# Value products in groups of four key blocks, and one more step ahead of the transposition of the row maxima

## The chip, the cores and the metric

The kernel is written directly for the engines of one core of a Trainium2 chip. The metric is the time of one launch on the device in microseconds; 2396.0 us is the median of three runs before the change (2391.77 to 2398.43).

## The reference

One layer of a decoder block over 2048 tokens of width 1024. Two attention branches read the same normalised input, each is gated, projected, weighted and summed. What matters here is the dense part of both branches, cut to its core:

```python
def mla_attention(q, k, v):                    # branch A: 8 heads, 96 wide, values 64 wide
    sc = einsum('bqhd,bkhd->bhqk', qb, k) * scale
    sc = where(causal, sc, -inf)
    p = softmax(sc, axis=-1)
    return einsum('bhqk,bkhd->bqhd', p, v)

def dsa_attention(q, k, v, q_idx, k_idx, w_idx, k_top):   # branch B: 8 heads, 2 key heads, 64 wide
    score = einsum('bqhs,bqh->bqs', relu(q_idx . k_idx), w_idx)
    _, sel = top_k(where(causal, score, -inf), 256)
    p = softmax(q . k[sel] * scale)            # over the 256 selected keys
    return p . v[sel]
```

The kernel does not gather in branch B: it computes all scores of a query block and adds a mask that is very negative where a key was not selected.

## The kernel before

The first 1106 us project the tokens, score and search the 256 keys, and write queries, keys, values and gates to device memory. The last 388 us merge the branches and apply the output projection. The change lies between them, in the attention.

**Units.** Attention is cut into 32 units in the hand-written order `UNITS` (line 38). A unit is one branch, one pair of heads (p, 0 to 3) and one group of 512 queries (g, 0 to 3). It has `nk` = 4g + 4 key blocks of 128 keys, 4 to 16; in all there are 320 blocks. For a block, `scores_t` (lines 629 to 680) computes for each of the two heads the transposed scores `st` (128 keys by 512 queries, three products in branch A, two in branch B, and bf16 products that add masks), ScalarE takes the exponential into `pt` (line 672), and the sum of the exponentials is kept in `acc` by an addition on GpSimd for the first head and on VectorE for the second (line 679). The last four blocks of a unit lie on the diagonal, so they are 512, 384, 256 and 128 columns wide.

**Value products.** `values` (line 682) multiplies `pt` with the values into `o`. It is two matmuls for a block, one for each head, and each head fills 64 of the 128 output rows, so that two of them run beside each other. A profile shows each such matmul as two records. They are not issued with their block: `scores_t` hands them to a list, and `flush` (lines 740 to 752), which is called inside every block after its first score products (`between`), issues them later, in groups. Three tiles in PSUM hold `st`, three hold `ap` (below) and two hold `o`.

**The end of a unit.** `finish` (line 689) multiplies `o` with the gate on VectorE, and sums `acc` over its 128 rows by two matmuls with ones on TensorE (line 698), for which both heads' last additions must be done. `flush` calls it after the value products, so many acting flushes after the unit's end as `AGE` says.

**Maxima.** The softmax subtracts a row maximum that is known before the unit begins. For each unit, `row_max` (line 590) computes the scores a second time the other way round, in 8(g + 1) pieces of up to 512 keys: a product `ap` on TensorE (line 600), then a maximum over it on VectorE (line 604, in branch B line 607), then for each of 8 rows of results a negation into `nm` (line 614). `shifts` (line 616) then transposes `nm` on TensorE (line 623), and ScalarE copies it and sends it by DMA into the last row of `Q` or `Q2`, where the score products pick it up.

**The order.** TensorE's order is exactly the order in which this code emits instructions (`manual_schedule`); the other engines' queues are ordered by a scheduler. While a unit runs, `fill` (line 760) gives out pieces of the next two or three units between the score products, by a rate that spreads them over the blocks that are left. A `yield` in `row_max` or `shifts` ends one step; `left` counts a unit's steps, 8(g + 1) + 2 of them: the pieces, the step that ends the last row's maximum, and the transposition. The steps of units 0 and 1 are taken in `project_tail` (line 1147), 28 of them, between the last products of the projection.

Of the kernel before, what the change touches and what calls it, by code (L numbers as in the profile page):

```python
# [28 lines left out]
SELECTED = -4.0e30  # L29
TOPK = 256  # L30
TARGET = 248.0
AGE = 1
X_BUFS = 3
X_AHEAD = 4
FIRST_GEMMS = [(0, 0), (0, 1), (0, 2), (1, 0), (0, 3), (1, 1), (0, 4), (0, 5), (1, 2), (0, 6), (1, 3), (0, 7), (1, 4), (1, 5), (1, 6), (1, 7)]
# [11 lines left out]
TAIL = 3  # L47
WAIT = 0
LEAD = 6
PT_BUFS = 10  # L50
WINDOW = 8.5
EVALS = 5
PAIRS = [(NT - 1 - n, 2 + n) for n in range(7)]
# [18 lines left out]
class Block:  # L72
# [543 lines left out]
    def shifts(self, g, q, k, mask, dst):  # L616
        nc, hd = self.nc, self.hd
        nm = hd.tile([P, 2, 4], F32, name="nm", tag="nm", bufs=3)
        for hh in range(2):
            yield from self.row_max(g, q(hh), k(hh), mask, nm[:, hh])  # L620
        yield
        ps = self.ps.tile([P, 512], F32, name="ap", tag="ap", bufs=3)
        nc.tensor.transpose(ps[0:8, 0:P], nm.rearrange("p a b -> p (a b)"), self.ident)
        nmT = hd.tile([8, P], F32R, name="nmT", tag="t8", bufs=2)
        nc.scalar.activation(nmT, ps[0:8, 0:P], AF.Copy)
        nc.scalar.dma_start(dst.bitcast(F32), nmT.bitcast(F32))
        yield

    def scores_t(self, u, j, fill, between):
# [18 lines left out]
        for hh in range(2):  # L648
# [21 lines left out]
            ps = banks[hh]  # L670
            pt = at.tile([P, 512], F32, name="pt", tag="pt", bufs=PT_BUFS)
            nc.scalar.activation(pt[:, n0:], ps[:, n0:], AF.Exp, scale=u["scale"])  # L672
# [41 lines left out]
    def pipeline(self, units, ahead):  # L714
        count = len(units)
        heads, spec, left = [None] * count, [None] * count, [0] * count
        begun, born, clock = 0, [0] * count, [0]

        def begin(n):
            nonlocal begun  # L720
            while begun < count and begun - ahead[begun] <= n:
                m = begun
                heads[m] = units[m]()
                spec[m] = next(heads[m])
                left[m] = 8 * (spec[m]["g"] + 1) + 2
                born[m] = clock[0]
                begun += 1

        def take(n):
            left[n] -= 1  # L730
            next(heads[n])

        begin(-1)
        for n in range(2):
            while left[n]:
                take(n)
                yield
        values, after = [], []

        def flush(keep=1):  # L740
            nonlocal after
            if keep and len(values) < 3:
                return
            while len(values) > keep:
                f, u, j = values.pop(0)
                f(u, j)
            rest = []
            for age, f, u in after:
                again = (age - 1, f) if age else f(u)
                if again is not None:  # L750
                    rest.append((again[0], again[1], u))
            after = rest

        for n in range(count):
            begin(n)
            u = spec[n]
            credit = [0.0]
            for j in range(u["nk"]):

                def fill(half):  # L760
                    slots, pieces, rate = 2 * (u["nk"] - j) - half - LEAD, 0, 0.0
                    for m in range(n + 1, begun):
                        pieces += left[m]
                        rate = max(rate, pieces / max(slots, 1))
                        slots += 2 * spec[m]["nk"]
                    credit[0] += rate
                    for m in range(n + 1, begun):
                        while left[m] and credit[0] >= 1.0 and clock[0] >= born[m] + WAIT:
                            take(m)
                            credit[0] -= 1.0  # L770

                clock[0] += 1
                values.append((self.scores_t(u, j, fill, flush), u, j))
            after.append((AGE, self.finish, u))
            while n + 1 < count and left[n + 1]:
                take(n + 1)
        while values or after:
            flush(0)
# [466 lines left out]
```

## Time and profile before

| what | value |
|---|---|
| median of three runs | 2396.0 us |
| the profiled execution | 2390.5 us, of that 2388.7 us from the first to the last instruction |
| TensorE busy | 2271.3 us (95%) |
| VectorE / GpSimd / ScalarE busy | 1446.3 us (61%) / 1317.2 us (55%) / 992.1 us (42%) |
| granted TensorE clock | 0.987 of full speed over the span |
| attention | from about 1106.6 to 2000.6 us |

Durations below come from this one execution. A matmul's record lasts longer than its share of TensorE, since matmuls overlap; the share is read from start to start. PE is TensorE's matmul side, PEld its weight loads, DVE VectorE, ACT ScalarE, POOL GpSimd. In a timeline equal instructions that follow each other are merged into one row (x8 are eight records), and the number in brackets is the idle time of the engine before it and what ended it.

### The profile page before, as it was taken

To read this page: it belongs to the slowest core of one execution; us is meant where nothing else is said; L and a number is where in the kernel's file an instruction comes from. 1 tells how busy PE (TensorE), PEld (TensorE's weight loads), DVE (VectorE), ACT (ScalarE), POOL (GpSimd) and SP (SyncE) were. 2 spreads that over 40 slices of the span, in tenths; PEclk is the share of its full clock that TensorE was granted. 3 is DMA by queue.
4 is the path that set the end of the run, shared out by engine and by line. 5 is a ranking of instruction groups with operands and counts; after the bars stand their busy time and mean duration, and the time that the engine had idled before them with its cause. 6 is when DMAs were issued, how large, how long until landed. Compare 5 with 4: busy or idle time off the path is not lost.

```text
span 2388.7 us, 38186 instructions
## 1 busy us (share of the span) xinstructions
PE 2271.3 (95%) x12882; PEld 1759.2 (74%) x12882; DVE 1446.3 (61%) x3296; ACT 992.1 (42%) x2002; POOL 1317.2 (55%) x1733
## 2 busy tenths in 40 slices
PE   7999999999988999899999999999999999999999
PEld 6999988877777777786565655656655556888888
DVE  6453525698686887866676676677778763222222
ACT  5342325766657667442344434434434443111110
POOL 5876958866666767643344434334765445433431
PEclk9999999999999999999999999999999999999999
DMA  9441333443448434448433322211313103444432
GB/s 308 140 144 52 122 109 127 147 153 115 155 145 253 149 115 153 132 143 243 139 103 100 116 72 63 68 53 59 95 50 98 32 14 101 143 145 137 128 125 84
DMA packets 298102, 288.39 MB, mean 121 GB/s; under 512 B 23408, under 2 KB 240880, under 8 KB 297776
## 3 DMA queue, kind: packets, MB, share of 16 engines
q1 hardware_dynamic: 297392, 285.81, 38.8%
q8 instruction: 101, 1.65, 0.3%
q14 instruction: 97, 0.79, 0.1%
q10 hardware_dynamic: 512, 0.13, 0.0%
HBM read 171.62 MB, written 114.10 MB: 120 GB/s over the span
## 4 chain that ended last, share of the span: by engine, by line
PE 51%; DVE 12%; DMA 8%; issue 5%; POOL 5%; ACT 4%; SPq 2%; DVEq 0%; ACTq 0%; POOLq 0%
PE st L646 17%; PE o L686 10%; PE ap L600 5%; DMA out_dram<-mx 4%; PE acc L113 3%; PE acc L114 3%; DVE sc L392 3%; PE acc L115 3%; ACT junk L439 2%; PE br L113 2%; PE br L115 1%; PE br L114 1%; PE st L698 1%; DMA mo<-d_o 1%; ACT zr L389 1%
## 5 line engine op out<-in xcount | busy, mean ns | idle before, releaser
L679 POOL TENSOR_TENSOR acc<-acc,pt 128x512 f32<-128x512 f32 (+3 forms) x288 | 327.3, 1137 | 361.1 <-ACT pt L672 350.0
L672 ACT ACTIVATE pt<-st 128x512 f32<-128x512 f32 (+3 forms) x640 | 339.6, 533 | 433.5 <-PE st L646 385.0
L392 DVE SCALAR_TENSOR_TENSOR sc<-zr,w_i,sc 128x512 f32<-128x512 f32 (+3 forms) x266 | 227.9, 859 | 98.4 <-ACT zr L389 94.8
L646 PE MATMUL st<-Q,K 96*128 96x512 f32 (+3 forms) x960 | 264.9, 383 | 0.5 <-ACT ev L352 0.5
L607 DVE CUSTOM_DVE_ANT_0 mj<-ap,mask 128x512 bf16<-128x512 f32 (+2 forms) x320 | 193.7, 605 | 102.4 <-PE ap L600 93.8
L604 DVE TENSOR_REDUCE mx<-ap 128x1 f32<-128x512 f32 (+2 forms) x320 | 185.3, 604 | 109.8 <-PE ap L600 64.5
L679 DVE TENSOR_TENSOR acc<-acc,pt 128x512 f32<-128x512 f32 (+3 forms) x288 | 218.7, 759 | 51.1 <-ACT pt L672 46.4
L646 PEld LDWEIGHTS st<-Q,K 96*128 96x128 f32 (+1 forms) x960 | 163.2, 191 | 73.2 <-issue 50.8
L389 ACT ACTIVATE zr<-z 128x512 f32<-128x512 f32 (+3 forms) x304 | 161.7, 544 | 90.1 <-PE z L387 85.7
L113 PE MATMUL acc<-hT0h,wfh 128*128 128x512 f32 x384 | 155.8, 406 | 8.4 <-ACT pqk L560 6.4
L113 PE MATMUL acc<-hT1h,wfh 128*128 128x512 f32 x384 | 157.7, 411 | 5.8 <-DMA hT1h<-d_h 2.9
L108 POOL TENSOR_SCALAR wfh<-wst 128x256 fp32r<-128x256 f32 x192 | 91.4, 490 | 123.2 <-DMA wst<-in_w_f 64.9
L109 POOL TENSOR_TENSOR wfl<-wst,wfh 128x256 fp32r<-128x256 f32 x192 | 157.1, 835 | 3.1
L114 PE MATMUL acc<-hT1l,wfh 128*128 128x512 f32 x384 | 153.4, 400 | 0.8 <-DMA hT1l<-d_h 0.8
L115 PE MATMUL acc<-hT1h,wfl 128*128 128x512 f32 x384 | 153.2, 399 | 0.0
L114 PE MATMUL acc<-hT0l,wfh 128*128 128x512 f32 x384 | 151.8, 395 | 1.0 <-DMA hT0l<-d_h 1.0
L115 PE MATMUL acc<-hT0h,wfl 128*128 128x512 f32 x384 | 151.7, 395 | 0.0
L686 PE MATMUL o<-pt,V 128*64 128x512 f32 (+3 forms) x640 | 135.9, 546 | 0.0
L686 PE MATMUL o<-pt,Vb 128*64 128x512 f32 (+3 forms) x640 | 134.5, 541 | 0.0
L646 PE MATMUL st<-Q,Kd 128*128 128x512 f32 (+3 forms) x320 | 133.0, 416 | 0.0
L907 DVE TENSOR_TENSOR sg<-br,sg 128x256 f32<-128x256 f32 x128 | 53.5, 423 | 128.4 <-PE br L115 72.1
L106 ACT ACTIVATE mh<-sg 128x256 fp32r<-128x256 f32 x64 | 26.7, 416 | 251.6 <-POOL sg L909 251.5
(283 smaller groups left out, 6101.1 us busy)
## 6 DMA issues: line engine op xcount, KB each, us to landing
wst<-in_w_f SPq DMA_DIRECT2D x192, 128.0 KB
d_f<-ev SPq DMA_DIRECT2D x96, 256.0 KB
sg<-d_f SPq DMA_DIRECT2D x128, 128.0 KB
d_q<-phl SPq DMA_DIRECT2D x32, 384.0 KB
d_k<-phl SPq DMA_DIRECT2D x32, 384.0 KB
K<-d_k SPq DMA_DIRECT2D x64, 192.0 KB
Q<-d_q SPq DMA_DIRECT2D x64, 192.0 KB
x<-in_x SPq DMA_DIRECT2D x16, 512.0 KB
```

Source lines behind the costliest of these rows:

```text
L109: (eng_lo or eng).tensor_tensor(lo, src, hi.bitcast(F32), op=OP.subtract)
L113: mm(ps, lhi, rhi, start=start, stop=False)
L114: mm(ps, lhi, rlo, start=False, stop=False)
L115: mm(ps, llo, rhi, start=False, stop=stop)
L389: nc.scalar.activation(r[:, :n], z[:, :n], AF.Relu)
L392: nc.vector.scalar_tensor_tensor(sc[:, k0:k0 + n], r[:, :n], ws, sc[:, k0:k0 + n], op0=OP.mult, op1=OP.add)
L604: nc.vector.tensor_reduce(mx[:, b:b + 1], ps[:, :n], axis=AX, op=OP.max)
L607: nc.vector.tensor_tensor_reduce(out=junk[:, :n], in0=ps[:, :n], in1=mask[i][:, 512 * b:512 * b + n], scale=1.0, scalar=-3.0e38, op0=OP.su ...
L646: nc.tensor.matmul(banks[hh][:, cols], l, r, start=start and n == 0, stop=stop and n == len(seq) - 1)
L672: nc.scalar.activation(pt[:, n0:], ps[:, n0:], AF.Exp, scale=u["scale"])
L679: eng.tensor_tensor(acc[:, n0:], acc[:, n0:], pt[:, n0:], op=OP.add)
L686: self.nc.tensor.matmul(u["o"][64 * hh:64 * hh + 64, n0:], u["v"](hh, j), pts[hh][:, n0:], start=(j == 0), stop=(j == u["nk"] - 1))
```

## The change

`flush` acts once more than four blocks are in the list, instead of three, and again leaves one; so it issues four blocks' value products in a row instead of two, at every fourth block. `AGE` goes from 1 to 0: `finish` follows in the same flush the value products of the unit's last block. There are 13 tiles `pt` instead of 10. `shifts` has one more empty step between the end of the last maximum and the transposition, and `left` counts it.

```diff
-AGE = 1
+AGE = 0
-PT_BUFS = 10
+PT_BUFS = 13
+GROUP = 4
@@ shifts
             yield from self.row_max(g, q(hh), k(hh), mask, nm[:, hh])
         yield
+        yield
         ps = self.ps.tile([P, 512], F32, name="ap", tag="ap", bufs=3)
         nc.tensor.transpose(ps[0:8, 0:P], nm.rearrange("p a b -> p (a b)"), self.ident)
@@ pipeline, begin
-                left[m] = 8 * (spec[m]["g"] + 1) + 2
+                left[m] = 8 * (spec[m]["g"] + 1) + 3
@@ pipeline, flush
-            if keep and len(values) < 3:
+            if keep and len(values) <= GROUP:
                 return
             while len(values) > keep:
                 f, u, j = values.pop(0)
                 f(u, j)
```

All line numbers of the changed program are one or two higher (line 600 is 601, 686 is 688, 698 is 700). In its order TensorE has 80 runs of value products, where there were 160. Three places show how its queue moves.

The first is TensorE's queue in the last quarter of a unit of branch A with 16 blocks, ahead of the transposition for the next unit (`o<-pt,V` are value products, `ap<-K,Q` a piece, `ap<-ident,nm` the transposition). Before:

```order
L600 MATMUL ap<-K,Q 128x512
L602 LDWEIGHTS identb
L602 MATMUL ap<-trib,identb 128x128
L646 MATMUL st<-Q,K 128x512
L686 MATMUL o<-pt,V 64x512 x4
L646 MATMUL st<-Q,K 128x512 x5
L623 MATMUL ap<-ident,nm 8x128
L646 MATMUL st<-Q,K 128x512 x3
```

The same place in the changed program:

```order
L601 MATMUL ap<-K,Q 128x512
L603 LDWEIGHTS identb
L603 MATMUL ap<-trib,identb 128x128
L648 MATMUL st<-Q,K 128x512 x9
L625 MATMUL ap<-ident,nm 8x128
L648 MATMUL st<-Q,K 128x512 x3
```

The transposition stands three score products further from the last piece than it did, and the value products that stood between them have gone to another block. Of the 32 transpositions, 8 had value products between the last piece and themselves; now 2 have.

The second place is TensorE's queue at the end of a unit of four blocks in branch A (`st<-acc,ones` are the sums of `finish`). Before, the unit's last value products (64x256 and 64x128) stood fourteen rows higher than the first sum, and the sums stood behind the next unit's first value products:

```order
L600 MATMUL ap<-K,Q 128x512
L646 MATMUL st<-Q,K 128x512
L686 MATMUL o<-pt,V 64x512 x4
L698 MATMUL st<-acc_14482,ones 64x512
L698 MATMUL st<-acc_14483,ones 64x512
L646 MATMUL st<-Q,K 128x512 x2
```

Now the four blocks' products and the sums are one run, in the second block of the next unit:

```order
L601 MATMUL ap<-K,Q 128x512
L648 MATMUL st<-Q,K 128x512
L688 MATMUL o<-pt,V 64x512 x2
L688 MATMUL o<-pt,V 64x384 x2
L688 MATMUL o<-pt,V 64x256 x2
L688 MATMUL o<-pt,V 64x128 x2
L700 MATMUL st<-acc_14477,ones 64x512
L700 MATMUL st<-acc_14478,ones 64x512
L648 MATMUL st<-Q,K 128x512
```

The sums have moved two blocks forward, right behind the unit's own last value products.

The third place is TensorE's queue at the seam between projection and attention (`acc<-hT1h,wfh` and its like are products of the projection). Before:

```order
L600 MATMUL ap<-K,Q 128x512 x2
L602 LDWEIGHTS identb
L602 MATMUL ap<-trib,identb 128x128
L113 MATMUL acc<-hT1h,wfh 128x512
L114 MATMUL acc<-hT1l,wfh 128x512
L115 MATMUL acc<-hT1h,wfl 128x512
L113 MATMUL acc<-hT1h,wfh 128x512
L114 MATMUL acc<-hT1l,wfh 128x512
L115 MATMUL acc<-hT1h,wfl 128x512
L623 MATMUL ap<-ident,nm 8x128
```

In the changed program:

```order
L115 MATMUL acc<-hT1l,wfh 128x512
L116 MATMUL acc<-hT1h,wfl 128x512
L601 MATMUL ap<-K,Q 128x512
L603 LDWEIGHTS identb
L603 MATMUL ap<-trib,identb 128x128
L625 MATMUL ap<-ident,nm 8x128
L648 MATMUL st<-Q,K 128x512 x3
```

`project_tail` still takes 28 steps, while units 0 and 1 now have 30; the pieces move back by one step, and the transposition for unit 1 follows its last piece at once.

## Rows read from the trace of the kernel before

**Rows 1.** The page's first line.

```profile
span 2388.7 us, 38186 instructions
```

**Rows 2.** Busy time by stretch: the attention, from its first to its last matmul.

```profile
core 0: us, PE busy (x) PEld busy (x) DVE busy (x) ACT busy (x) POOL busy (x), PEclk, DMA share, GB/s
1106.60:2000.60 894.00, 872.96 (x4982) 527.38 (x4984) 624.73 (x1690) 367.03 (x705) 419.85 (x397) 1.00 0.27 78
```

**Rows 3.** TensorE's waits in the attention: in total, times, longest (us).

```profile
PE ap L623 <- DVE nm L614: 15.4, 17, 2.2
PE ap L600 <- DVE mx L607: 3.1, 6, 0.8
```

**Rows 4.** Timeline (start, us), a group of value products in branch B.

```profile
1426.53 0.51 PE L646 MATMUL st<-negb,mask 128*128 128x128 bf16 x6
...
1426.97 1.94 PE L686 MATMUL o<-pt,Vb 128*64 128x512 f32 x8
...
1428.83 0.19 PEld L646 LDWEIGHTS st<-Q,Kd 128*128 128x128 f32 x1 [0.81 <-issue]
1428.84 0.44 PE L646 MATMUL st<-Q,Kd 128*128 128x384 f32 x1
```

**Rows 5.** Timeline, a block without value products, then one with, and its sums.

```profile
1415.01 0.61 PE L646 MATMUL st<-negb,mask 128*128 128x128 bf16 x8
...
1415.43 0.48 PE L646 MATMUL st<-Q,Kd 128*128 128x512 f32 x1
...
1415.75 0.40 PE L646 MATMUL st<-Q,Kl 65*128 65x512 f32 x1
...
1417.70 1.94 PE L686 MATMUL o<-pt,Vb 128*64 128x512 f32 x8
...
1419.47 1.03 PE L698 MATMUL st<-acc,ones 128*64 128x512 f32 x4
...
1420.43 0.50 PE L646 MATMUL st<-Q,Kd 128*128 128x512 f32 x1
...
1420.76 0.40 PE L646 MATMUL st<-Q,Kl 65*128 65x512 f32 x1
```

**Rows 6.** All value products of line 686: duration ns shortest/median/longest, starts, forms.

```profile
L686 PE MATMUL o<-pt,V x640: 272/592/1061, 1113.7 to 1694.2; 128*64 128x512 f32 x112, 128*64 128x384 f32 x16, 128*64 128x256 f32 x16, 128*64 128x128 f32 x16
...
L686 PE MATMUL o<-pt,Vb x640: 272/592/645, 1340.1 to 2000.2; 128*64 128x512 f32 x112, 128*64 128x384 f32 x16, 128*64 128x256 f32 x16, 128*64 128x128 f32 x16
```

**Rows 7.** Timeline, from a last piece to its transposition, value products between.

```profile
1209.10 0.39 PE L600 MATMUL ap<-K,Q 96*128 96x512 f32 x1
...
1211.10 0.15 DVE L614 TENSOR_SCALAR nm<-mx 128x1 f32<-128x1 f32 x1
1211.64 1.45 PE L646 MATMUL st<-Q,K 96*128 96x512 f32 x5
...
1212.92 0.27 PE L623 MATMUL ap<-ident,nm 128*8 128x128 f32 x1
```

**Rows 8.** Timeline at the seam: unit 1's last piece and its last maximum.

```profile
1104.09 0.23 PE L602 MATMUL ap<-trib,identb 128*128 128x128 bf16 x1
...
1105.57 0.15 DVE L614 TENSOR_SCALAR nm<-mx 128x1 f32<-128x1 f32 x1
```

**Rows 9.** Timeline around the end of unit 24 (branch B, 12 blocks).

```profile
1725.53 0.87 PE L686 MATMUL o<-pt,Vb 128*64 128x256 f32 x8
...
1731.35 2.13 POOL L679 TENSOR_TENSOR acc<-acc,pt 128x128 f32<-128x128 f32 x2
...
1732.31 1.08 PE L698 MATMUL st<-acc,ones 128*64 128x512 f32 x4
```

**Rows 10.** Busy time by stretches of four blocks: three of the 80.

```profile
1146.50:1159.70 13.20, 13.20 (x59) 7.50 (x58) 10.57 (x23) 5.37 (x9) 5.13 (x4) 1.00 0.61 183
...
1717.70:1726.60 8.90, 8.90 (x65) 6.08 (x64) 7.24 (x26) 3.57 (x8) 8.90 (x9) 1.00 0.32 87
...
1934.30:1946.50 12.20, 12.20 (x77) 7.41 (x75) 10.13 (x34) 4.78 (x8) 5.14 (x5) 1.00 0.01 1
```

**Rows 11.** Busy time within the 80 groups that the change moves, summed.

```profile
sum 138.54, PE 138.54 PEld 44.22 DVE 116.40 ACT 29.17 POOL 72.01; mean PE 1.73 PEld 0.55 DVE 1.45 ACT 0.36 POOL 0.90
```

## The prediction

> **What bounds the kernel now.** I read the busy times by stretch first: the attention takes 894 of the 2388.7 us, TensorE is busy in 873 of them at the full granted clock (1.00), VectorE in 625, GpSimd in 420, ScalarE in 367 [rows 1, 2]. So in the part that changes TensorE sets the pace, and the order in which its instructions stand is the time. Then the list of its waits: of some 21 us of idleness, 15.4 us are spent ahead of the transposition, in 17 waits of up to 2.2 us, and 3.1 us ahead of pieces that wait for a free `ap` tile [rows 3]. VectorE has 30% of slack over the whole, which is less than it looks, because it is not spread evenly (below). So I look for what TensorE itself does less of, and then for waits that come in its place.
>
> **Fewer switches.** No matmul is added or taken away. What goes is 80 of the 160 places at which TensorE changes from score products to value products and back: 1280 records of value products [rows 6] in runs of eight. The timeline prices a switch. Into a group: eight masks occupy 0.42 us up to the next score product, some 54 ns each, while six masks ahead of value products occupy 0.44 instead of 0.33 us: +0.11 [rows 4, 5]. Inside and out: a pass of 512 columns takes 0.43 us (two passes of the sums, 1419.47 to 1420.43, take 0.96, the way out included); the four passes of a group that is followed by the sums take 1.77, those of one that is followed by scores take 1.87 us: some 0.05 at the start and 0.10 at the end [rows 4, 5]. After it, the second score product starts 0.33 us after the first, not 0.235 (five products in 1.28 us with that first gap in them, [rows 7]): +0.10. That is 0.36 us. Against it stands that masks followed directly by scores also cost a gap, 0.32 us instead of 0.235 from the first score product to the second, though these masks overlap the first [rows 5]; taken off, 0.27 remains. In branch A without masks nothing is taken off. I take 0.33; 80 × 0.33 = 26 us, ends 22 and 29. Nothing hides a switch, as TensorE waits for nothing there, so the 26 us come off the path that sets the end.
>
> The Trainium skill has a rule that speaks against this term: by "TensorE: Matmul & The Clock Gate" (section "Architectural detail: the array is 16× 32×32, not 1× 128×128") the queue pulls weight loads ahead of matmuls in flight, and by that alone a switch would be free and the term nothing. Here the load for the first score product starts 0.01 us ahead of it, after 0.81 us in which the loader did nothing [rows 4], so at these places the trace does not agree; "TensorEngine Tiling (Array Packing)", section "Key Properties", says that a change of tiling mode drains the engine, which fits.
>
> **The extra step.** It is meant for the 15.4 us, but it competes with the grouping. In the new order each transposition gets between nothing and 1.9 us more score products ahead of it, mostly 0.3 to 1.0; taken off the 17 waits that would be about 7 us. But 8 transpositions had a group of value products (1.73 us on average, [rows 11]) between the last piece and themselves, and now only 2 have. In the row shown, the last piece starts at 1209.10 and its maximum is ready at 1211.25, 2.15 us later, and TensorE arrives at 1212.92 without waiting; with nine products of 0.235 us between, it arrives after some 2.3 us: just covered [rows 7]. Others of these six have less cover, 1.5 to 2.3 us; I put 3 us on them. At the seam the transposition now follows its last piece directly, and from that piece to the last maximum 1.63 us pass [rows 8], a new wait of 1.5 us. And VectorE will be later in the longer stretches without value products, perhaps 4 us over all. Sum: −7 + 3 + 1.5 + 4, about +2 us; ends −10 (nearly all waits gone) and +12 (each transposition 0.4 us later).
>
> **The earlier sums.** They wait for the last additions on both adders. In the units I followed in the timeline, these end before the unit's own last value products do, so the two blocks less cost nothing. Unit 24 is the exception: GpSimd splits the branch weights at the same time and is busy without a pause (8.90 of 8.90 us, [rows 10]). Its last addition, 128 columns wide, is the first of the two of the row at 1731.35, and cannot be done before that; the sums came at 1732.31. In the new order they stand behind the value products that ended at 1725.53 + 0.80 = 1726.3, and TensorE arrives there about 1 us earlier, as three switches of this unit are gone [rows 9]. GpSimd's queue holds the same instructions ahead of that addition. So TensorE waits for it: 1731.8 less 1725.3, some 6 us, once; ends 0 (if the scheduler's other order of the splits frees it) and 7. What is queued behind the sums waits with them: all of TensorE, and so ScalarE and VectorE, which lose nothing that counts.
>
> **Longer bursts.** This is what I can't read off a row. Between groups there are now four blocks instead of two. The 80 groups that move away are 138.5 us long, and VectorE works in 116.4 us of them [rows 11]: there it catches up on the pieces that TensorE has put out faster than they are reduced. TensorE can run ahead by three `ap` tiles only. In the cycle of 13.20 us that the first row shows VectorE works 10.57 us [rows 10]. With two groups of 1.73 us and their switches TensorE has 9.1 us of scores and pieces in it. Placed in one stretch, VectorE has some 10 us to do against 9.1, starts half a microsecond late, and ends about 1.5 us behind: two pieces, which three tiles hold. Where it is busier, they do not. In 13 of the 80 cycles VectorE works over 80% of the time; the first and the last of them stand in the rows, 1146.50 and 1934.30 [rows 10]. A cycle can lose at most the moved group, 1.73 us. If only these 13 lose, and all they can, it is 22 us; if the tiles hold throughout, nothing; if every cycle loses 0.5 us, 40. I take 9 us, two thirds of a microsecond in each of the 13, nearer to the 3.1 us of waits of this kind that there are now [rows 3]. The 13 `pt` tiles hold the five blocks that may now stand in the list (ten tiles) and three more, so ScalarE does not wait for them.
>
> **Sum.** −26 + 2 + 6 + 9 = −9 us. On the profiled execution 2390.5 becomes 2381.5; the median shown is 5.5 us above that execution, and I carry the difference over: 2396.0 − 9 = 2387 us. That is 0.4%, and what a measurement of this kernel can tell from no change is about 0.3%, 7.2 us.
>
> **The rivals.**
>
> A. The bursts cost nothing and the transpositions win: −26 − 7 (or −10) and at most 2 for unit 24, up to −33, 2363 us. For it: on average VectorE's excess fits into three tiles. Against it: the 13 busy cycles, and the lost cover of six transpositions, which is in the order.
>
> B. The grouping is nearly paid back: bursts cost 16 us instead of 9, −2, 2394 us: no change. For it: TensorE now has hardly a wait on pieces, so there may be little reserve beyond the two-block rhythm.
>
> C. Slower: VectorE becomes the engine that TensorE waits for in each burst. The mechanism has one place, the product `ap` that finds its three tiles full, one price, 0.5 us in each of 80 cycles, 40 us, and one point from which it decides: when these waits exceed some 25 us, the switches are paid back. −26 + 2 + 6 + 40 = +22, 2418 us. For it: VectorE uses 84% of the moved groups' time [rows 11]. Against it: the merged group is twice as long, and VectorE catches up there.
>
> D. Fewer switches bring nothing: the gaps at a group belong to its length and not to its ends, and the loads of the next weights are ready in any case. Then the first term is 0, and 0 + 2 + 6 + 9 = +17, 2413 us. For it: the gaps are small and read from few rows. Against it: each of the four is seen at a switch and not between passes [rows 4, 5]. This is what the rule on weight loads that the Trainium skill's page "TensorE: Matmul & The Clock Gate" states (section named above) would make of the change.
>
> **How the numbers follow.** The forecast, −15 to −3 us around −9, has 0.44; two thirds of it are beyond 7.2 us, so 0.30 faster and 0.14 same. A has 0.20, faster. B has 0.16, same. C has 0.14 and D 0.06, slower. Faster 0.50, same 0.30, slower 0.20. The range from 2366 to 2409 takes most of A and the lower half of the slower cases; the likeliest case's own range is 2381 to 2393.
>
> **What would show it.** TensorE's start-to-start gaps at value products: half as many switches, each 0.33 us. The list of waits: the transposition at 10 to 20 us, pieces `ap` at 5 to 15 us, and one wait of about 6 us of the sums for GpSimd's addition near 1725. If pieces wait over 25 us, C was right; if under 3 us, A. The attention should be 885 us long instead of 894, and the stretches ahead of it and behind it as before. If these differ by more than 2 us, something moved that I did not see, such as the larger `pt` pool pushing other tiles to places that are still in use.

## The result, and the profile after

The changed kernel takes 2420.4 us (median of nine runs, 2407.3 to 2429.3) where the kernel before, run on the same chip, takes 2398.4 (nine runs, 2391.8 to 2403.2). The ratio is 1.0083, 95% interval 1.006 to 1.0106: slower by 0.8%. The forecast was 2387, 9 us less than before; measured are 22 us more (by the medians), which is beyond the range.

The page's first lines; the span answers to [rows 1]:

```profile
span 2418.6 us, 38237 instructions
## 1 busy us (share of the span) xinstructions
PE 2276.7 (94%) x12882; PEld 1768.5 (73%) x12882; DVE 1433.6 (59%) x3296; ACT 994.8 (41%) x2002; POOL 1319.5 (55%) x1733
```

The profiled execution lasted 2420.4 us, and its granted clock is 0.978 over the span (before 0.987). The attention by stretch, which answers to [rows 2], and below it the first and the last of the eight stretches in it with a granted clock of 0.50, and one between:

```profile
core 0: us, PE busy (x) PEld busy (x) DVE busy (x) ACT busy (x) POOL busy (x), PEclk, DMA share, GB/s
1107.50:2035.20 927.70, 882.58 (x4986) 540.38 (x4985) 611.80 (x1690) 368.98 (x705) 421.00 (x397) 0.97 0.25 75
1114.30:1127.90 13.60, 13.60 (x45) 8.43 (x45) 7.59 (x22) 2.52 (x6) 2.99 (x5) 0.50 0.72 206
...
1725.30:1732.10 6.80, 6.22 (x27) 4.03 (x29) 3.23 (x8) 1.95 (x4) 6.80 (x6) 0.50 0.38 94
...
1988.10:1991.50 3.40, 3.40 (x14) 1.37 (x14) 0.00 (x0) 0.75 (x2) 0.99 (x1) 0.50 0.01 1
```

The attention is 33 us longer (927.7; 894.7 from the first score product to the first product of the merge). The part ahead of it ends 0.9 us later, and the unchanged end takes 383.4 instead of 387.4. In the runs here this end took 383 to 396 us, so I read nothing from that. The same view over the eight stretches alone sums them:

```profile
sum 54.50, PE 49.57 PEld 27.31 DVE 25.68 ACT 11.11 POOL 21.86; mean PE 6.20 PEld 3.41 DVE 3.21 ACT 1.39 POOL 2.73
```

TensorE ran 54.5 us at the lower of its two levels, 1.2 GHz, and was busy in 49.6 of them. Before, one such stretch lay in the attention:

```profile
1134.20:1137.60 3.40, 3.40 (x10) 1.11 (x7) 0.67 (x2) 0.23 (x1) 1.00 (x1) 0.50 0.53 154
```

The waits in the attention of the changed kernel, which answer to [rows 3]:

```profile
PE ap L625 <- DVE nm L615: 31.4, 21, 2.9
PE ap L601 <- DVE mx L608: 11.3, 16, 4.4
PE st L648 <- ACT pt L674: 1.7, 1, 1.7
```

The transposition waits 31.4 us (before 15.4), the pieces 11.3 (before 3.1). One of the 21, start to end, from the timeline of TensorE, VectorE and GpSimd:

```profile
1720.43 0.40 PE L648 MATMUL st<-Q,Kl 65*128 65x512 f32 x1
...
1720.68 0.40 PE L601 MATMUL ap<-Kd,Q 128*128 128x512 f32 x1
...
1722.05 0.69 DVE L608 CUSTOM_DVE_ANT_0 mj<-ap,mask 128x512 bf16<-128x512 f32 x1
...
1722.27 1.28 POOL L681 TENSOR_TENSOR acc<-acc,pt 128x512 f32<-128x512 f32 x1
...
1722.61 0.39 PE L648 MATMUL st<-Q,Kl 65*128 65x512 f32 x1
...
1722.67 1.43 DVE L681 TENSOR_TENSOR acc<-acc,pt 128x512 f32<-128x512 f32 x1
...
1723.50 1.72 POOL L110 TENSOR_TENSOR wb0l<-wst,wb0h 128x512 fp32r<-128x512 f32 x1
1724.02 0.68 DVE L608 CUSTOM_DVE_ANT_0 mj<-ap,mask 128x512 bf16<-128x512 f32 x1
...
1724.81 0.95 DVE L681 TENSOR_TENSOR acc<-acc,pt 128x512 f32<-128x512 f32 x1
...
1725.69 0.14 DVE L615 TENSOR_SCALAR nm<-mx 128x1 f32<-128x1 f32 x1
...
1725.88 0.38 PE L625 MATMUL ap<-ident,nm 128*8 128x128 f32 x1 [2.89 <-DVE nm L615]
...
1727.45 0.63 PE L648 MATMUL st<-Q,Kl 65*128 65x512 f32 x1
...
1727.87 0.63 PE L601 MATMUL ap<-Kd,Q 128*128 128x512 f32 x1
```

TensorE stops at 1723.0 and starts at 1725.88. When the last piece has been put out (1721.1), VectorE still has this one and the two before it to reduce, and among these and the last negation stand two additions for the second head (`acc`, 1.43 and 0.95 us): the negation has to pass both. Each addition ends some 0.6 us after GpSimd's instruction does that was running when it began (1723.55 and 1724.10; 1725.22 and 1725.76); with GpSimd idle such an addition takes 0.68 us in all (1865.29, two fences below). The Trainium skill, "SBUF — State Buffer" (section "SBUF: two separate sides"), says that a VectorE instruction with two inputs in SBUF and a GpSimd instruction that reads SBUF shut each other out for their whole length. The two ends here agree with that; no run took GpSimd's instructions away to test it. The clock falls at 1725.3, within this wait, and behind it a product of 512 columns takes 0.42 us (1727.45 to 1727.87) where it took 0.25 before the wait (1720.43 to 1720.68). The same shape, an addition right ahead of the last negation, stands at 1139, where the clock did not fall:

```profile
1138.03 1.20 DVE L681 TENSOR_TENSOR acc<-acc,pt 128x512 f32<-128x512 f32 x1 [0.34 <-ACT pt L674]
1139.15 0.14 DVE L615 TENSOR_SCALAR nm<-mx 128x1 f32<-128x1 f32 x1
```

The longest wait of a piece has another cause, the reciprocal of the denominators:

```profile
1862.65 0.94 DVE L713 RECIPROCAL li<-li 32x128 f32<-32x128 f32 x1 [4.55 <-DMA li<-d_l]
...
1864.26 0.80 PE L601 MATMUL ap<-Kd,Q 128*128 128x512 f32 x1 [4.44 <-DVE mx L608]
...
1865.29 0.68 DVE L681 TENSOR_TENSOR acc<-acc,pt 128x512 f32<-128x512 f32 x1
```

VectorE stood 4.55 us at the head of its queue until a DMA brought `li`, with pieces waiting behind. Before, its one such wait (4.8 us) fell at 2006, behind the attention.

The switches themselves did what was forecast. A group of four blocks, followed by scores (answers to [rows 4, 5]):

```profile
1485.43 3.65 PE L688 MATMUL o<-pt,V 128*64 128x512 f32 x16
1489.01 0.73 PE L648 MATMUL st<-Q,K 96*128 96x512 f32 x2
```

Four blocks take 3.58 us; twice the two blocks of before are 3.74. To see the whole attention I took, over all starts of TensorE in it, what each interval exceeds its columns at 2.4 GHz by, and sorted these by what follows what (own sums over both traces, stretches at 1.2 GHz apart). From value products to scores 33.0 us became 14.8, from masks to value products 11.0 became 4.7, from scores to value products 6.3 became 3.0, from value products to sums 6.4 became 1.6. Less what the value products show among themselves (10 us more), that is 22 us less; the rest, mostly between score products, makes it some 25. Against it stand +25 in the stretches at 1.2 GHz, +14.5 ahead of the transpositions, and +18 around pieces. −25 + 25 + 14.5 + 18 = +32.5, of the 33 measured. Every interval is in one of these parts, so they must add up: the sum says where the time lies, not why. Of the 18 only some 8 are listed waits (3.9 became 11.7, three releasers); the rest are gaps too short for the list, which I did not take apart.

These 33 us are those of two single executions. The one of the kernel before took 2390.5 us, 8 less than its median here, and had a granted clock of 0.987, where the median of its runs beside the experiments is 0.984 to 0.985; the one of the changed kernel is its median, at 0.978. So the pair shows 30 us of difference where the medians show 22. From the clocks alone, 0.985 less 0.978 of some 2400 us, I estimate 17 us for the clock's part between the medians, where this pair gives 25.

### The profile page after: what moved, and what is told of

Same layout as the page of the kernel before. It is cut to its first block, busy times and chain, and to the rows that moved or that the text cites. A ratio compares the mean times of both kernels' runs of the same rounds, so it can differ in the third digit from the quotient of the medians.

```text
span 2418.6 us, 38237 instructions
## 1 busy us (share of the span) xinstructions
PE 2276.7 (94%) x12882; PEld 1768.5 (73%) x12882; DVE 1433.6 (59%) x3296; ACT 994.8 (41%) x2002; POOL 1319.5 (55%) x1733
## 4 chain that ended last, share of the span: by engine, by line
PE 52%; DVE 14%; issue 6%; DMA 6%; ACT 5%; POOL 3%; SPq 2%; ACTq 0%; DVEq 0%; POOLq 0%
PE st L648 15%; PE o L688 11%; PE ap L601 5%; DVE sc L393 3%; PE acc L114 3%; PE acc L115 3%; PE acc L116 3%; DVE mj L608 2%; DMA out_dram<-mx 2%; ACT junk L440 2%; PE br L114 2%; PE br L116 2%; PE br L115 2%; PE ou L116 2%; PE ou L115 2%
## 5 line engine op out<-in xcount | busy, mean ns | idle before, releaser
L393 DVE SCALAR_TENSOR_TENSOR sc<-zr,w_i,sc 128x512 f32<-128x512 f32 (+3 forms) x266 | 232.8, 877 | 102.2 <-ACT zr L390 98.4
L648 PE MATMUL st<-Q,K 96*128 96x512 f32 (+3 forms) x960 | 259.8, 384 | 1.7 <-ACT pt L674 1.7
L601 PE MATMUL ap<-Kd,Q 128*128 128x512 f32 (+2 forms) x320 | 120.6, 390 | 12.2 <-DVE mx L608 11.3
L688 PE MATMUL o<-pt,V 128*64 128x512 f32 (+3 forms) x640 | 130.6, 551 | 0.0
L388 PE MATMUL z<-kT,iqT 128*128 128x512 f32 (+3 forms) x304 | 112.2, 373 | 18.6 <-ACT zr L390 18.4
```

The costliest lines, as they stand in the source:

```text
L393: nc.vector.scalar_tensor_tensor(sc[:, k0:k0 + n], r[:, :n], ws, sc[:, k0:k0 + n], op0=OP.mult, op1=OP.add)
L601: nc.tensor.matmul(ps[:, :n], q[:, i * P:(i + 1) * P], k(b)[:, :n], start=True, stop=not diag)
L648: nc.tensor.matmul(banks[hh][:, cols], l, r, start=start and n == 0, stop=stop and n == len(seq) - 1)
L688: self.nc.tensor.matmul(u["o"][64 * hh:64 * hh + 64, n0:], u["v"](hh, j), pts[hh][:, n0:], start=(j == 0), stop=(j == u["nk"] - 1))
```

## The experiments

Each ratio is against the kernel before, run in turn on the same chip, with its 95% interval. The order is that in which they ran.

**The step alone, and the grouping without it.** Kernel before, with the step:

```diff
         yield
+        yield
         ps = self.ps.tile([P, 512], F32, name="ap", tag="ap", bufs=3)
...
-                left[m] = 8 * (spec[m]["g"] + 1) + 2
+                left[m] = 8 * (spec[m]["g"] + 1) + 3
```

> The kernel before with nothing but the extra step ahead of the transposition. If the waits come from VectorE falling behind in the longer stretches between groups (theory V): the waits ahead of the transposition fall from 15.7 us to about 8, the clock falls as seldom as before (under 10 us at 1.2 GHz in the attention), and the time is 2390 us, 8 below before. If the extra step is itself what costs (theory S): 2410 us or more.

Measured: 2393.4 us, 0.9961 (0.9942 to 0.9979).

```profile
PE ap L600 <- DVE mx L607: 3.8, 7, 0.8
PE ap L624 <- DVE nm L614: 2.8, 6, 1.3
```

```profile
1111.70:1139.00 27.30, 27.30 (x83) 16.54 (x84) 13.94 (x35) 5.40 (x11) 6.40 (x8) 0.50 0.57 167
```

By itself the step does what it is meant for: the waits at the transposition nearly vanish. Yet at the seam, where the transposition now follows its piece directly, TensorE waits 1.25 us for VectorE at 1105.5 and 1.88 for ScalarE's exponential at 1110.9, and then runs 27.3 us at 1.2 GHz (second fence, busy throughout). This profiled execution is the longest of the ten: 2402.4 us at a clock of 0.979, where the medians are 2393.4 and 0.984. So a stretch of this length is not what most of them have.

The changed kernel with those lines undone:

> The changed kernel without the extra step: groups of four, the earlier sums and 13 pt tiles remain. Theory V: the waits ahead of the transposition grow from the 30 us of the changed kernel to 35 to 45, with 50 us or more at 1.2 GHz; 2420 to 2435 us. Theory S: back to 2396 us or below.

Measured: 2428.8 us, 1.0137 (1.0083 to 1.019).

```profile
PE ap L624 <- DVE nm L615: 40.6, 23, 3.3
```

So it is the grouping (with `AGE` and `pt`) that costs, and the step takes part of that back: 9 us of waits at the transposition (40.6 to 31.4). In time the two kernels' intervals overlap.

**Without the second head's additions.** In both kernels VectorE's additions to the second head's softmax sum are left out, all but the first block's:

```diff
-                eng.tensor_scalar(acc, pt, 1.0, 0.0, op0=OP.mult, op1=OP.add)
-            else:
+                eng.tensor_scalar(acc, pt, 1.0, float(hh), op0=OP.mult, op1=OP.add)
+            elif hh == 0:
```

> The kernel before without VectorE's additions to acc for the second head (all blocks but the first; the first block's sum for that head starts from one), so the second head's softmax sum is left out. VectorE has some 200 us less to do in the attention. Theory V: waits ahead of the transposition about 5 us, no other change, 2386 us.

> The changed kernel without the same additions of VectorE (the second head's softmax sum is left out). Theory V: with VectorE free of them the longer stretches no longer make it late, waits and clock are as in the kernel before without these additions, and the fewer switches show alone: 25 us less than that kernel, about 2361 us. If longer runs of value products themselves lower the clock (theory P): 40 us or more at 1.2 GHz in the attention remain, and the time is within 10 us of the kernel before without the additions.

Measured: 2382.9 us, 0.9925 (0.99 to 0.9951) for the kernel before, and 2366.0, 0.9836 (0.9792 to 0.9881) for the changed one.

```profile
1108.50:1977.00 868.50, 857.33 (x4985) 536.70 (x4984) 442.56 (x1402) 366.35 (x705) 402.86 (x397) 0.98 0.27 80
```

```profile
PE ap L625 <- DVE nm L615: 4.4, 5, 1.3
PE ap L601 <- DVE mx L608: 4.1, 2, 3.7
PE st L700 <- POOL acc L681: 2.1, 1, 2.1
```

With VectorE relieved (442.6 us of work for 611.8) the same order of TensorE is 17 us faster than the old one, not 22 slower. This is the experiment that settles the engine: the groups pay for themselves, and what eats the gain passes through VectorE. The clock is less clear: 27.3 us at 1.2 GHz are left here, where the kernel before without these additions had 10.2. Each of the four stretches stands at or behind a wait of 1.2 to 3.7 us, half of the time at the seam. That runs twice as long do not lower the clock by themselves is shown by the last experiment, with the same runs and 3.4 us at 1.2 GHz.

**The seam.** The pieces of units 0 and 1 get as many steps as these units now have, in the kernel with the step alone and in the changed kernel:

```diff
-        slots, done, count = 8 * TAIL, 0, 28
+        slots, done, count = 8 * TAIL, 0, 30
```

> The kernel before with the extra step, and with 30 instead of 28 steps taken in project_tail, so that unit 1's last piece and its transposition do not meet at the seam. If the 27 us at 1.2 GHz right behind the seam (1111.7 to 1139.0 in the kernel with the step alone) come from the two waits there (theory M), they are gone, and the time is 8 to 14 us below the kernel with the step alone: 2382 us. If the clock falls there anyway (theory N: it falls at the change from projection to attention): 2393 us.

Measured: 2390.5 us, 0.9968 (0.9952 to 0.9984). The stretch at the seam is gone in the profile (6.8 us at 1.2 GHz in the attention for 34.1), but by time it can't be told from the step alone (0.9961), whose profile was its longest execution.

> The changed kernel with 30 instead of 28 steps taken in project_tail. Theory M: the 13.6 us at 1.2 GHz behind the seam are gone, the other waits stay; 8 us below the changed kernel, 2412 us. Theory N: 2420 us.

Measured: 2425.9 us, 1.0115 (1.007 to 1.0161). The time is missed: the stretch at the seam is gone here too, but the clock falls elsewhere.

```profile
1111.70:1125.30 13.60, 13.42 (x72) 8.88 (x71) 10.99 (x31) 5.29 (x12) 8.37 (x8) 1.00 0.80 239
...
1171.00:1174.40 3.40, 3.40 (x13) 1.25 (x13) 0.45 (x2) 0.50 (x2) 0.99 (x1) 0.50 0.22 61
```

```profile
1170.43 0.27 PE L625 MATMUL ap<-ident,nm 128*8 128x128 f32 x1 [1.98 <-DVE nm L615]
```

The wait of 1.98 us at 1170.4 is followed by a stretch at 1.2 GHz. In the changed kernel the same transposition waits the same 1.98 us and no stretch follows it:

```profile
1176.38 0.27 PE L625 MATMUL ap<-ident,nm 128*8 128x128 f32 x1 [1.98 <-DVE nm L615]
```

In all 51.2 us at 1.2 GHz remain, where there were 54.5. As long as the waits stand, the seam alone wins nothing.

**More steps.** The changed kernel with two more empty steps, `left` and the seam to match:

```diff
         yield
+        yield
+        yield
...
-                left[m] = 8 * (spec[m]["g"] + 1) + 3
+                left[m] = 8 * (spec[m]["g"] + 1) + 5
...
-        slots, done, count = 8 * TAIL, 0, 28
+        slots, done, count = 8 * TAIL, 0, 34
```

> The changed kernel with the seam mended and two more empty steps ahead of each transposition (three instead of one; 34 steps in project_tail). Theory V with the clock as its consequence: the waits ahead of the transposition fall from 30 us to about 5, the time at 1.2 GHz from 55 to under 20, the waits for free ap tiles (13 us) stay; 2385 us. If the clock falls by the longer runs (theory P): the waits fall, 40 us or more at 1.2 GHz stay, 2405 us.

Measured: 2394.8 us, 0.9988 (0.9974 to 1.0003).

```profile
PE ap L601 <- DVE mx L608: 11.2, 20, 4.4
PE ap L627 <- DVE nm L615: 6.9, 12, 0.9
PE st L702 <- POOL acc L683: 4.4, 1, 4.4
```

The transposition's waits fall to 6.9 us, none over 0.9, the stretches at 1.2 GHz to 17.1 us, and 31 us come back of the kernel with the seam alone (26 of the changed one): the time is that of the kernel before. The pieces' waits are untouched, and the predicted wait of unit 24's sums appears.

**Half of the additions on GpSimd.** With 30 steps at the seam, every other addition of the second head moves:

```diff
-            eng = nc.vector if hh and j else nc.gpsimd
+            eng = nc.vector if hh and j % 2 else nc.gpsimd
```

> The changed kernel with the seam mended and with every second addition of the second head (even key blocks) on GpSimd instead of VectorE; the sum is the same. VectorE is relieved of some 100 us in the attention, GpSimd gets some 150. Theory V: waits ahead of the transposition and for ap tiles halve to about 20 us together, 2390 us. If GpSimd becomes the engine that is waited for: waits of the score products for exponentials (ACT waiting for pt tiles), 2415 us.

Measured: 2393.1 us, 0.9988 (0.9969 to 1.0007).

```profile
PE st L700 <- POOL acc L681: 11.8, 1, 11.8
PE ap L625 <- DVE nm L615: 10.1, 14, 1.4
```

Nearly the same gain by another way to the same waits, less the 11.8 us that the busy GpSimd makes TensorE wait once, at unit 24.

**The sums' place alone.** Kernel before:

```diff
-AGE = 1
+AGE = 0
```

> The kernel before with nothing but AGE = 0: groups of two, the sums follow the unit's own last value products. If the earlier sums cost by themselves (theory E): a wait of about 6 us of the sums for GpSimd at unit 24 and waits elsewhere, 2403 us or more. If the cost lies in the grouping alone (theory V): one wait of 4 to 7 us at unit 24, else as before, within 5 us of before.

Measured: 2403.4 us, 1.0021 (1.0001 to 1.0041).

```profile
PE st L698 <- POOL acc L679: 4.3, 1, 4.3
PE ap L600 <- DVE mx L607: 4.2, 4, 2.9
```

The wait at unit 24 is real, 4.3 us, and so is a second cost: VectorE meets the reciprocal's DMA early here as well (6.9 us in two waits). The waits at the transposition are as before (15.4 us in 17), but 27.3 us ran at 1.2 GHz; this profiled execution is the longest of ten, 2413.6 us, so that figure is a high one.

**A fourth tile for pieces.** In the changed kernel `ap` gets a fourth tile in PSUM, and `o` keeps one of two; the pool is closed a little earlier so that its banks fit:

```diff
-        ps = self.ps.tile([P, 512], F32, name="ap", tag="ap", bufs=3)
+        ps = self.ps.tile([P, 512], F32, name="ap", tag="ap", bufs=4)
...
-            u["o"] = self.pp.tile([P, 512], F32, name="o", tag="o", bufs=2)
+            u["o"] = self.pp.tile([P, 512], F32, name="o", tag="o", bufs=1)
```

> The changed kernel with four tiles ap and one tile o (the earlier sums make one enough), eight banks of PSUM as before. If full ap tiles are the place where TensorE loses to VectorE (rival C of the prediction): most of the loss goes, 2400 us. Theory V as the runs so far put it (the transposition is the place): the 13 us of waits for ap tiles fall under 5, but the transposition waits longer than 30 us, since one more piece can lie ahead of its own; 2412 to 2420 us.

Measured: 2404.5 us, 1.0028 (1.0006 to 1.0049).

```profile
PE ap L625 <- DVE nm L615: 34.1, 21, 2.9
PE ap L601 <- DVE mx L608: 2.0, 5, 0.6
```

The pieces' waits nearly vanish and some 16 us come back (13 by the ratios); the transposition's waits and 61.4 us at 1.2 GHz remain. That separates the two places at which VectorE is late. One tile `o` instead of two is part of this run and was not tried by itself.

**All of it.** The three steps; half the additions on GpSimd, except in units 24 and 25; one half of the branch weights' split on ScalarE, so that GpSimd is free there:

```diff
-            eng = nc.vector if hh and j else nc.gpsimd
+            own = j % 2 or u["branch"] and u["g"] == 2 and u["p"] < 2
+            eng = nc.vector if hh and j and own else nc.gpsimd
...
-                                       ((nc.gpsimd, nc.gpsimd),)) for b in range(2)]
+                                       ((nc.scalar, nc.gpsimd),)) for b in range(2)]
```

> A version that is to keep the gain of the grouping: groups of four, three empty steps ahead of the transposition and 34 steps at the seam, every second addition of the second head on GpSimd except in units 24 and 25, and the first half of the split of the branch weights on ScalarE, which relieves GpSimd at unit 24. Theory V: waits ahead of the transposition under 5 us, for ap tiles under 10, at unit 24 under 3, the clock at 1.2 GHz for under 10 us; 2372 us. If the work moved to GpSimd and ScalarE is paid for elsewhere: 2390 us.

Measured: 2391.3 us, 0.9965 (0.9947 to 0.9984). Short of what was expected.

```profile
PE ap L601 <- DVE mx L608: 14.3, 21, 3.8
PE ap L627 <- DVE nm L615: 3.9, 6, 1.1
```

The transposition is settled, the pieces still wait, and 30.7 us ran at 1.2 GHz where under 10 were expected. 13.6 of them lie right behind the seam, though no transposition waits there any more; ahead of them TensorE waits 1.36 us for ScalarE. So mending the seam does not by itself keep the clock up. The last experiment is this kernel with four `ap` tiles and one `o`:

> The version e11_all with four tiles ap and one tile o besides. The waits for ap tiles, under 10 us there, fall under 4; 2367 us. If the waits for ap tiles only move to the transposition: no better than e11_all.

Measured: **2373.7 us, 0.9903 (0.9872 to 0.9933)**, faster than both kernels.

```profile
1107.60:1978.70 871.10, 853.05 (x4984) 528.14 (x4984) 554.80 (x1572) 374.71 (x721) 539.30 (x499) 1.00 0.27 80
```

```profile
PE ap L627 <- DVE nm L615: 7.1, 10, 1.1
PE ap L601 <- DVE mx L608: 4.9, 11, 0.8
```

The attention takes 871.1 us instead of 894.7, at a mean granted clock of 1.00. That is 23.6 less, near the 26 that the switches were priced at; but 8 us fewer waits at the transposition than before (7.1 for 15.4) are in it too. 3.4 us ran at 1.2 GHz, as before the change.

## Why the prediction was wrong

**The switches** were priced well: some −22 to −25 us against −26 in the sum, 3.58 us for a group where twice 1.87 less 0.15 was forecast; and −17 us of gain where both kernels are without the additions, at a median clock of 0.983 against 0.985. (The −24 of all of it hold other gains too.) Rival D, that they bring nothing, falls.

**The extra step** is the first term that failed. It was put at +2 us, −10 to +12. Alone it is worth −6 us by the medians, −9 by the ratio (0.9961). Beside the grouping the waits at the transposition rose by 16 us. The step's own part was right: it takes 9 us of waits off (40.6 to 31.4), and 7 were forecast. What failed is the other part, what the grouping adds to these waits: 25 us without the step (15.4 to 40.6), where 3 for lost cover and 4 for VectorE's lateness stood in the sum. "VectorE will be later in the longer stretches without value products, perhaps 4 us over all" was the sentence that had the mechanism and not its size. I priced VectorE's lateness as a sum over the stretch, and did not read what stands ahead of the last negation in VectorE's own queue: additions of the second head, 0.95 and 1.43 us in the wait shown, made longer by GpSimd's work beside them. What shows it is the kernel without them: 31.4 us become 4.4.

**Longer bursts** were put at +9 us, 0 to 22, 40 at the worst. The listed waits for a free tile rose by 8, 4.4 of them in a single wait on a DMA that the term did not contain, and the gaps around pieces by 18 in all; a fourth tile brings 13 to 16 back. So the term was about half its size.

**The earlier sums** were put at +6. In the changed kernel nothing waits there, as TensorE arrives late itself (the wait of 2.9 us at 1725.9 and 1.2 GHz up to 1732.1). The mechanism is there: 4.3 us with `AGE` alone, 4.4 with more steps, 11.8 with more additions on GpSimd. The reciprocal, which also moves with `AGE`, was not in the sum.

**What was left out** is the largest: TensorE's clock. The sum took all of the attention at the full granted clock, since [rows 2] had 1.00, and priced each wait by its own length. In the changed kernel's profile 49.6 us of work ran at 1.2 GHz; half of it, an estimated 25 us, would not have been there at 2.4 (some 17 between the medians, as estimated above). That is about what the switches give. A wait of 2 us was priced at 2 us; with 16 us more of them at the transposition came 51 us more at the lower clock. Their sum alone does not decide it: the kernel before had 15.4 us of them and one short stretch. But waits of 1.2 us and more were 4 in its attention, and 17 in the changed kernel's.

**The rivals.** C came nearest: 2418 us, with VectorE as the engine that TensorE waits for. But its place was the `ap` tile and its price 40 us of waits there; measured are 11.3 there, 31.4 at the transposition, and the clock behind both. So its time is right in part by accident. A named no wait that grew. B's price for the bursts, 16 us, is near the 18 measured around pieces, but it kept the transposition at +2 and the full clock.

**What stays open.** Why one wait of 1.98 us is followed by a stretch at 1.2 GHz and an equal one is not (1170.4 and 1176.4 above) no run here settles. The Trainium skill, "TensorE: Matmul & The Clock Gate" (section "What's actually happening"), says that the gate's own rhythm is not tied to a kernel's start; that would fit, as would the nine executions of the changed kernel, with mean clocks from 0.973 to 0.982, but no run tests it. The share of `AGE` and of the groups within the loss was not fully parted: `AGE` alone costs 0.2%, the groups without it were not run, and neither were the 13 tiles `pt` by themselves. VectorE waits for `o` 56.3 us in the changed kernel and 15.6 before; the fastest kernel keeps 43.2 us of it, so it can't be the main cause, but it was not tried by itself. With three `ap` tiles all the cures together win no more than the step alone (0.9965 and 0.9961); that a fourth tile mends this is shown, why the pieces' waits were as long as in the changed kernel is not.

## What to carry to other kernels

Making an engine's runs longer changes when its partner is loaded: read the partner's queue at the one instruction that the next stage waits for (here the last negation), not its mean load. Where TensorE is the bound, price a wait of one to three microseconds at more than its length: in the changed kernel's trace the stretches at 1.2 GHz cost an estimated 25 us beside 43 us of waits at the transposition and the pieces; in the trace before, with few long waits, 2 us beside 18.5. Before you read the clock of one profile, compare that execution with the median of its runs: here two were 8 and 10 us below it, and two 9 and 10 above. A regrouping that loses can still be right: look for what it makes late, relieve that, and measure both kernels with that engine relieved.

## What was not expected of the hardware

- At or behind waits of 1.2 to 4.4 us in otherwise dense work the granted clock was 0.50 in stretches of 3.4 to 27.3 us. A few short ones had only shorter waits ahead, such as 0.44 us in the run with three steps (3.4 us from 1404.0). At the seam of the kernel with the step alone TensorE was busy for 27.30 of 27.30 us and still had 0.50. Idle time does not order the runs: with four `ap` tiles TensorE sat idle 38.6 us in the attention and 61.4 us ran at 1.2 GHz; with half of the additions on GpSimd 33.2 and 20.5. The number of waits of 1.2 us and more, counted in the traces, orders them better: 15 and 6 in these two, with 11 and 2 stretches; 17 and 8 in the changed kernel, 4 and 1 in the kernel before, 2 and 1 in the fastest.
- In the runs of the changed kernel the time follows the clock: 2407.3 us at a mean granted clock of 0.981, 2429.3 at 0.973.
